# Preparing a recurrent segment inside the scan of the one before it, with both directions' outputs in one PSUM bank

## The chip, the cores and the metric

One core of one Trainium2 chip. The metric is device microseconds (us) of one execution; the time before is the median of 3 runs.

## The reference, cut to what matters

Two layers of a hybrid backbone, float32. Each layer: adaLN (`silu(c) @ w_ada`), one input projection `h @ w_in` for 256 context and 256 latent tokens, three head groups (retention, latent attention MLA, RWKV-7), and an output projection with LayerNorm. The change concerns RWKV-7, which runs in both directions:

```python
def step(state, inp):                      # per direction, head; state (v, k)
    r_t, w_t, k_t, v_t, a_t, b_t = inp     # a = -kk, b = kk * a_rate
    sa = einsum('dbhvk,dbhk->dbhv', state, a_t)
    state = state * w_t[..., None, :] + sa[..., :, None] * b_t[..., None, :] \
          + v_t[..., :, None] * k_t[..., None, :]
    return state, einsum('dbhvk,dbhk->dbhv', state, r_t)
```

The inputs need `tanh`/`exp` of two low-rank products (`w_lora`, `a_lora`), a unit key `kk / |kk|`, and cumulative products of the decay. The result is normalised per head.

## The kernel before, in words

TensorE (PE) runs in program order; the instructions of the other engines are put in order by a scheduler, which takes what is ready.

**Mainline.** All large projections (`pm`, L447; `acc`, L1311) and the 64 adaLN pieces (`adap`, L403, each with a load of 1 MB, tag `raw2`) form one list of pieces. A load brings `raw` (256 KB), ACT rounds it to `whi` (L225), POOL or DVE subtracts the rest `wlo` (L226), and PE multiplies three times. `ahead` runs ahead of PE in that list: `NRAW` = 10 pieces are loaded ahead (7 buffers), `NHI` = 4 of them split, and one adaLN piece more than the one in use (`raw2` has 2 buffers). The mainline is also PE's filler: `M(name)` adds the credit `FILL[layer][name]` (about us of PE time at the full clock) and issues mainline matmuls until it is used up. So filler moves matmuls from one place to another; their number stays.

**RWKV part.** For a layer, `rwkv_half` runs twice (4 of 8 heads each): unit keys (`sq`, `ss`, `nr`, with the reciprocal in L640), then two segments (context, latent), 8 segments in both layers. A segment has these steps:
1. Preparation, four units (direction d, head pair j): two matmuls `z`, four activations on ACT (`th`, `th`, `w`, `w`, L672 to L678), nine operations on DVE (two scans L681, `AR` L687 and L690 or L694, five that write `bf`, L698 to L705). Unit n+1 is emitted ahead of the gram of unit n, with filler `z0`, `gram`, `tp` between.
2. For each unit: `gram` matmuls (L711), mask to `G` on DVE (L714), `bs` on POOL (L718, one buffer), four transposes `bkT` (L723).
3. A block inverse on DVE: transposes to `Mt` (L747, copied by L148 on ACT), a chain of `stmp`/`S` pairs (L764, L767), transposes back, `TA` (L782), under filler `inv0` and `inv1`; then `pA`, `pB` on PE (L790).
4. The scan: 4 chunk steps, each a chain PE → ACT/DVE → PE: `xy` (L827, L846), copy `Y` (ACT, L148), `uz` (L852), copy `W`, `uz` (L861), new state `Zb` (DVE, L865 or L867), `xy` (L874); values of the next chunk (`uz` L816, `W` L820). `xy` and `uz` have a PSUM bank for each direction, which are all 4 banks of the pool `sm`.
5. Normalisation and output, deferred into the filler of the next segment (`norm`, `fin`).

Of the kernel before, what the change touches and what calls it, by code (L numbers as in the profile page):

```python
# [10 lines left out]
F32 = mybir.dt.float32  # L11
# [11 lines left out]
T = 512  # L23
# [114 lines left out]
def hybrid_kernel(ctx, tc, I, out, dbg=None, layers=L):  # L138
# [123 lines left out]
    def units():  # L262
        i = 0
        while True:
# [13 lines left out]
            ahead(i, loaded, False, NADA, lambda j: load(j, "raw2", NADA + 1))  # L278
# [341 lines left out]
    def rwkv_half(rp, l, hf, rF, kF, vF, twl, al, last):  # L620
        c0 = 2 * hf
        kkF = rp.tile([128, 2, T], F32, tag="kkF", name="kkF", bufs=1)
        w2t = rp.tile([128, 2, 256], F32, tag="w2t", name="w2t", bufs=1)
        for q, src in ((0, "rwkv_w2"), (1, "rwkv_a2")):
            nc.sync.dma_start(out=w2t[:, q, :],
                                in_=I[src][l].rearrange("d r c -> (d r) c")[:, 256 * hf:256 * hf + 256])

        M("begin")
        sq = []
        for j in range(2):  # L630
            sq.append(rp.tile([128, T], F32, tag="tb", name="sq", bufs=4))
# [12 lines left out]
        for d in range(2):
            for q in range(2):
                nc.gpsimd.memset(Zb[d][q], 0.0)
        Z = [None, None]
        for seg in range(2):
            need = not (last and seg == 0)
            NY = 128 if need else 64  # L650
            s0 = seg * NCTX
            AR, BK, G, pC = [], [], [], []
            Gt = rp.tile([128, 2, 4, 4, 128], F32, tag="G", name="G", bufs=1)
            for d in range(2):
                ar = rp.tile([128, 2, 4, 128], F32, tag="AR", name="AR", bufs=2)
                bk = rp.tile([128, 4, 2, 128], F32, tag="BK", name="BK", bufs=2)
                g = Gt[:, d]
                pc = rp.tile([128, 2, 4], F32, tag="pC", name="pC", bufs=2)
                AR.append(ar), BK.append(bk), G.append(g), pC.append(pc)
            def unit(d, j):  # L660
                ar, bk, g, pc = AR[d], BK[d], G[d], pC[d]
                mk = masks[:, d]
                fwd = (lambda ap: ap[:, ::-1]) if d else (lambda ap: ap)
                hp0 = 64 * d
                c = c0 + j
                cs = slice(j * 128, j * 128 + 128)
                sg = slice(s0, s0 + NCTX)
                z = pbank([128, 2, NCTX], "z")
                mm(z[:, 0], lhsT=w2t[hp0:hp0 + 64, 0, cs], rhs=twl[hp0:hp0 + 64, sg], start=True, stop=True)
                mm(z[:, 1], lhsT=w2t[hp0:hp0 + 64, 1, cs], rhs=al[hp0:hp0 + 64, sg], start=True, stop=True)  # L670
                th = rp.tile([128, 2, NCTX], F32, tag="tb", name="th", bufs=4)
                act(out=fwd(th[:, 0]), in_=z[:, 0], func=AF.Tanh, scale=0.5, bias=dpc(l, 14 + 4 * d + c))  # L672
                act(out=fwd(th[:, 1]), in_=z[:, 1], func=AF.Tanh, scale=0.5, bias=dpc(l, 22 + 4 * d + c))
                w = rp.tile([128, 2, 4, 65], F32, tag="w", name="w", bufs=2)
                nc.gpsimd.memset(w[:, :, :, 0], 0.0)
                thv = th[:, 0].rearrange("p (c t) -> p c t", t=64)
                act(out=w[:, 0, :, 1:65], in_=thv, func=AF.Exp, scale=-CDEC / 2, bias=val(0))
                act(out=w[:, 1, :, 1:65], in_=thv, func=AF.Exp, scale=CDEC / 2, bias=val(1))  # L678
                for q in range(2):
# [24 lines left out]
                TT(out=kx, in0=kx, in1=kn[:, ::-1, :] if d else kn, op=ALU.mult)
# [826 lines left out]
```

## Time and profile before

| | |
|---|---|
| Median of 3 runs (lowest, highest) | 2138.4 us (2136.77, 2141.34) |
| Profiled execution: time, span | 2137.61 us, 2135.8 us |
| PE, DVE, ACT, POOL busy | 92%, 60%, 38%, 29% |
| Mean granted TensorE clock | 0.949 of full speed |
| RWKV part of layer 0, layer 1 | 242 to 680 us, 1371 to 1810 us |

The profiled execution lies 0.8 us below the median; 1.8 us of it are outside the span. Busy shares are averages over stages with different limits.

### The profile page before, as it was taken

What the parts mean: (1) busy time and instruction counts of PE and PEld (TensorE: products, weight loads), DVE (VectorE), ACT (ScalarE), POOL (GpSimd) and SP (SyncE); (2) the same over time, 40 slices, a digit from 0 to 9 for tenths busy, and PEclk for the clock granted to TensorE, in tenths of its full rate; (3) what the DMA queues carried; (4) which work ended last, traced back from release to release, by engine and by line L of the source; (5) the groups of instructions that cost most, each with busy time, mean ns of one, the idle gap of its engine ahead of it and who ended that gap; (6) DMA issues with size and microseconds to landing.
All of it is one profiled execution on the core that took longest, in us unless ns stands there. A gap on an engine that the chain in (4) does not pass through costs nothing.

```text
span 2135.8 us, 35152 instructions
## 1 busy us (share of the span) xinstructions
PE 1959.7 (92%) x13046; PEld 1515.1 (71%) x13046; DVE 1273.4 (60%) x2985; ACT 813.1 (38%) x1559; POOL 611.3 (29%) x568
## 2 busy tenths in 40 slices
PE   6999999999989899999999979989798879899896
PEld 3567666676667577877877767766686668898775
DVE  2446876769493354446633374584749492466857
ACT  3223423343323344444322253423343234565442
POOL 0000433344243221112000055533444245513302
PEclk9999999999999999999999989978899889999998
DMA  9983442535243754536576533321322122743774
GB/s 338 352 272 98 143 141 71 163 114 173 75 148 106 256 160 124 158 104 231 183 249 230 179 104 108 99 55 31 87 75 80 39 75 74 206 111 111 237 242 157
DMA packets 255468, 318.42 MB, mean 149 GB/s; under 512 B 28288, under 2 KB 171968, under 8 KB 254400
## 3 DMA queue, kind: packets, MB, share of 16 engines
q1 hardware_dynamic: 255296, 316.16, 47.2%
q8 instruction: 103, 1.69, 0.3%
q14 instruction: 69, 0.57, 0.1%
HBM read 290.64 MB, written 25.46 MB: 148 GB/s over the span
## 4 chain that ended last, share of the span: by engine, by line
PE 46%; DVE 14%; ACT 2%; issue 1%; DMA 1%; POOL 0%; DVEq 0%; SPq 0%; ACTq 0%; POOLq 0%
PE pm L447 17%; PE acc L1311 11%; DVE stmp L764 2%; DVE S L767 2%; PE adap L403 1%; PE pj L344 1%; PE pj L343 1%; PE pj L342 1%; DVE H L583 1%; PE xy L827 1%; PE uz L852 1%; DVE G L772 1%; PE pmx L447 1%; PE gram L711 1%; PE pT L1123 1%
## 5 line engine op out<-in xcount | busy, mean ns | idle before, releaser
L447 PE MATMUL pm<-H,whi 128*128 128x512 f32 (+2 forms) x2880 | 853.6, 377 | 15.4 <-DVE stg L600 12.2
L226 POOL TENSOR_TENSOR wlo<-raw,whi 128x512 fp32r<-128x512 f32 x332 | 457.7, 1382 | 1078.1 <-ACT whi L225 992.0
L447 PEld LDWEIGHTS pm<-H,whi 128*128 128x128 f32 (+1 forms) x2880 | 520.7, 193 | 149.3 <-issue 43.3
L225 ACT ACTIVATE whi<-raw 128x512 fp32r<-128x512 f32 x556 | 348.9, 630 | 660.4 <-PE pm L447 316.7
L447 PE MATMUL pm<-H,wlo 128*128 128x512 f32 (+2 forms) x1440 | 541.3, 376 | 2.2 <-POOL wlo L226 2.2
L447 PEld LDWEIGHTS pm<-H,wlo 128*128 128x128 f32 (+1 forms) x1440 | 278.6, 193 | 57.6 <-issue 12.9
L226 DVE TENSOR_TENSOR wlo<-raw,whi 128x512 fp32r<-128x512 f32 x224 | 155.0, 695 | 201.5 <-ACT whi L225 162.5
L1311 PE MATMUL acc<-whi,Y 128*128 128x512 f32 x768 | 245.4, 399 | 5.0 <-DVE stg L600 4.6
L1311 PEld LDWEIGHTS acc<-whi,Y 128*128 128x128 f32 x768 | 143.3, 189 | 48.3 <-ACT whi L225 14.0
L1311 PE MATMUL acc<-wlo,Y 128*128 128x512 f32 x384 | 151.6, 395 | 0.0
L764 DVE TENSOR_TENSOR stmp<-S,Mt 128x60 f32<-128x60 f32 (+14 forms) x488 | 121.6, 289 | 6.5 <-ACT Mt L148 5.6
L767 DVE TENSOR_TENSOR S<-S,stmp 128x60 f32<-128x60 f32 (+14 forms) x488 | 108.0, 261 | 0.4
L447 PE MATMUL pmx<-H,whi 128*128 128x512 f32 (+1 forms) x256 | 87.1, 416 | 19.4 <-DVE H L583 13.0
L867 DVE TENSOR_TENSOR Zb<-Zc,uz 64x128 f32<-64x128 f32 x96 | 27.4, 286 | 126.1 <-PE uz L861 107.8
L1311 PEld LDWEIGHTS acc<-wlo,Y 128*128 128x128 f32 x384 | 72.5, 189 | 15.5 <-DVE wlo L226 0.4
L447 PEld LDWEIGHTS pmx<-H,whi 128*128 128x128 f32 x256 | 52.3, 215 | 37.5 <-DVE H L583 16.2
L148 ACT ACTIVATE Y<-xy 64x256 f32<-64x256 f32 x88 | 33.2, 377 | 118.5 <-PE xy L846 76.6
L403 PE MATMUL adap<-raw,scv 128*32 128x512 f32 x512 | 70.8, 626 | 0.0
L831 POOL TENSOR_TENSOR Zc<-Zb,pC 128x256 f32<-128x256 f32 x56 | 34.2, 615 | 118.0 <-DVE Zb L867 62.1
L711 PE MATMUL gram<-AR,bf 64*128 64x128 f32 (+1 forms) x512 | 42.9, 313 | 19.9 <-DVE bf L705 19.9
L711 PEld LDWEIGHTS gram<-AR,bf 64*128 64x128 f32 x512 | 36.8, 215 | 34.0 <-issue 21.3
L790 PE MATMUL pA<-TA,G 32*32 32x32 f32 x512 | 11.0, 237 | 54.0 <-DVE TA L782 54.0
(305 smaller groups left out, 2940.8 us busy)
## 6 DMA issues: line engine op xcount, KB each, us to landing
raw<-in_w_in SPq DMA_DIRECT2D x388, 256.0 KB, 2.8
raw<-in_w_ada SPq DMA_DIRECT2D x64, 1024.0 KB, 5.3
xraw<-in_w_ada SPq DMA_DIRECT2D x32, 1024.0 KB, 8.3
raw<-in_w_out SPq DMA_DIRECT2D x128, 256.0 KB, 4.0
raw<-in_mla_w_uq SPq DMA_DIRECT2D x48, 128.0 KB, 2.9
s_g<-stg SPq DMA_DIRECT2D x16, 256.0 KB, 3.1
gl<-s_g SPq DMA_DIRECT2D x16, 256.0 KB, 3.4
raw<-in_mla_w_ukv SPq DMA_DIRECT2D x32, 128.0 KB, 2.3
```

Of the source, the lines that this page charges most:

```text
L148: act(out=o, in_=i, func=AF.Copy)
L225: act(out=hi, in_=raw, func=AF.Copy)
L226: sub.tensor_tensor(out=lo, in0=raw, in1=hi.bitcast(F32), op=ALU.subtract)
L342: mm(ps, lhsT=ah, rhs=bh, start=first, stop=False)
L403: mm(st["ps"][32 * g:32 * g + 32, :], lhsT=sc(k + g), rhs=raw[:, g], start=(k == 0), stop=(k == KT - 4))
L447: mm(ps[p, i][:w], lhsT=x[:, o:o + w], rhs=H[y][:, a:], start=(k == k1 and n == 0), stop=(k == k2 - 1 and n == 2))
L711: mm(gps[p][:, i, :NY], lhsT=bf[hsl, i].rearrange("p a t -> p (a t)"), rhs=ar[hsl, j, i, :NY], start=True, stop=True)
L764: TT(out=tv, in0=S[:, r0:, s:s + 1].to_broadcast([128, n, b - a]), in1=Mt[s // 16][:, s % 16:s % 16 + 1, a:b].to_broadcast([128, n, b - a] ...
L767: TT(out=S[:, r0:, a:b], in0=S[:, r0:, a:b], in1=tv, op=ALU.add)
L831: nc.gpsimd.tensor_tensor(out=Zc[:, d], in0=Z[d], in1=pC[d][:, :, i:i + 1].to_broadcast([128, 2, 128]), op=ALU.mult)
L867: TT(out=Zn[hs(p), :, hs(p)], in0=Zc[hs(p), d, :, hs(p)], in1=zp[hs(p)], op=ALU.add)
L1311: mm(acc[cb, t], lhsT=Y[n][x][:, ts], rhs=y, start=(n == 0 and m == 0), stop=(n == KT - 1 and m == 2))
```

## The change

`rwkv` replaces both calls of `rwkv_half`. `prepare`, `grams`, `token_major`, `inverse_blocks`, `inverse_rest`, `scan`, `norm` and `finish` hold the code of the steps above. Only the first segment of a layer is prepared by itself. The four units of segment n+1 are emitted at hooks in the scan of segment n: within a half at A0, B0, B1, B2; between the halves at A1, B1, A2, B2, with the new half's `open_half` and `unit_keys` at S and A0. `norm` of a segment goes to A3 of the next scan. Hook A stands behind the copy `Y`, hook B behind `Zb` and `xy`.

To make a PSUM bank free for `z` and `ss` there, both directions' `xy` share one bank (`xyt`), and one copy of 64x512 (for two of 64x256) writes `Y` for both; so `uz` of either direction waits for both. `chain()` gives operations of the inverse and scan chains a higher priority in the scheduler. With `RP`, the second factor of `AR`, the last factor of `bf` and two operations of `norm` go from DVE to POOL. `bf` has 4 buffers of its own, `AR` and `pC` 4 (before 2), `Y` 2 (before 1); `NRAW` is 7 (4 buffers of `raw`), `raw2` has 1 buffer. The table `FILL` is new for the RWKV part.

```diff
 FILL = [
-    dict(zq=0.7, norm=2.34, end0=17.28, a0=3.38, a1=0.7, ada=2.41, begin=3.59, sq=2.6, nr=8.0, z0=3.35,
-         gram=1.84, tp=1.15, inv0=0.07, inv1=26.4, pA=1.2, pB=1.2, xy=0.39, u=0.44, zp=0.42, fin=15.02,
+    dict(zq=0.7, end0=17.28, a0=3.38, a1=0.7, ada=2.41, begin=3.59, sq=2.6, nr=8.0, z0=5.0,
+         gram=0.7, tp=0.4, inv0=0.07, inv1=29.0, pA=1.2, pB=1.2, xy=0.6, u=0.5, zp=0.5,
          kr=8.65, rss=3.69, rms=7.04, pj=1.74, rope=3.02, s0=5.05, s=0.47, av=1.41, s1=1.5, end=5.5, ret0=0.85,
          ret=2.09),
-    dict(zq=0.0, norm=11.89, end0=15.71, ada=6.79, begin=9.04, sq=1.32, nr=8.31, z0=4.0, gram=1.09, tp=0.1,
-         inv0=1.61, inv1=23.4, pA=1.2, pB=1.2, xy=0.68, u=0.39, zp=0.55, fin=4.57, kr=9.24, rss=1.71, rms=3.8,
+    dict(zq=0.2, end0=15.71, ada=6.79, begin=9.04, sq=1.32, nr=8.31, z0=5.0, gram=0.5, tp=0.3,
+         inv0=0.7, inv1=27.0, pA=1.2, pB=1.2, xy=0.68, u=0.45, zp=0.55, kr=9.24, rss=1.71, rms=3.8,
          pj=0.14, rope=2.75, s0=3.42, s=0.0, av=0.0, s1=0.49, end=0.82, ret0=0.45, ret=1.57),
 ]
-NRAW = 10
+NRAW = 7
+HPO = 300
+RP = True
 NHI = 4
...
-            ahead(i, loaded, False, NADA, lambda j: load(j, "raw2", NADA + 1))
+            ahead(i, loaded, False, NADA, lambda j: load(j, "raw2", 1))
...
+            STT(out=ar[:, j, :, 0:64], in0=Px, scalar=-1.0, in1=kkv, op0=ALU.mult, op1=ALU.mult)
+            PT = nc.gpsimd.tensor_tensor if RP else TT
+            if S.need:
+                if d == 0:
+                    PT(out=ar[:, j, :, 64:128], in0=Pi, in1=v4(rF[:, j, sg]), op=ALU.mult)
...
+            bf = S.bf[d, j] = rp.tile([128, 4, 2, 64], F32, tag="bf", name="bf", bufs=4)
...
+            PT(out=kx, in0=kx, in1=rn, op=ALU.mult)
...
+        def scan(S, hook):
+
+            rF, kF, vF = S.F
+            s0, need, AR, BK, pC = S.s0, S.need, S.AR, S.BK, S.pC
+            G = [S.G[:, d] for d in range(2)]
+            Y = S.Y = rp.tile([128, 4, 256], F32, tag="Y", name="Y", bufs=2)
             Yb = [rp.tile([128, 2, 256], F32, tag="tb", name="Yb", bufs=4) for n in range(2)] if need else None
             Zc = rp.tile([128, 2, 2, 128], F32, tag="bs", name="Zc", bufs=1)
-            hs = lambda h: slice(64 * h, 64 * h + 64)
-            xy = [pbank([128, 256], "xy") for d in range(2)]
+
+            xyt = pbank([128, 2, 256], "xy")
+            xy = [xyt[:, d] for d in range(2)]
...
+            hook("S")
...
-                    copy_a(Y[0:64, 2 * d + i % 2, :], xy[d][0:64])
+                                   start=False, stop=(d == 1 and j == 1 and r.start == 0))
+                with chain():
+                    copy_a(Y[0:64, i % 2::2, :], xyt[0:64])
+                hook(f"A{i}")
                 M("xy")
...
-                    copy_a(W[d][0:64], uz[d][0:64, 0:256])
+                    with chain():
+                        copy_a(W[d][0:64], uz[d][0:64, 0:256])
...
                 if i < 3:
+                    hook(f"B{i}")
                     M("zq")
...
+        def norm(S):
+            rF, kF, vF = S.F
+            Y, sg = S.Y, S.sg
+            yq = Y[64:128].rearrange("p c (h e) -> p (c h) e", e=64)
+            sm = rp.tile([128, 4, 16], F32, tag="gst", name="gst", bufs=1)
+            mean, var, rs = sm[64:128, 0], sm[64:128, 1], sm[64:128, 2]
+            PT = nc.gpsimd.tensor_tensor if RP else TT
+            nc.vector.tensor_reduce(out=mean, in_=yq, axis=AX.X, op=ALU.add)
+            TS(out=mean, in0=mean, scalar1=1.0 / 64, scalar2=None, op0=ALU.mult)
+            PT(out=yq, in0=yq, in1=mean.unsqueeze(2).to_broadcast([64, 16, 64]), op=ALU.subtract)
+            for n in range(0, 16, 8):
+                y2 = rp.tile([128, 8, 64], F32, tag="tb", name="y2", bufs=4)
+                act(out=y2[64:128], in_=yq[:, n:n + 8], func=AF.Square)
+                nc.vector.tensor_reduce(out=var[:, n:n + 8], in_=y2[64:128], axis=AX.X, op=ALU.add)
+            TS(out=var, in0=var, scalar1=1.0 / 64, scalar2=RW_EPS, op0=ALU.mult, op1=ALU.add)
...
+        M("begin")
+        open_half(0)
+        M("sq")
+        unit_keys(0)
+        M("nr")
+        S = Segment(0)
+        for d, j in ORDER:
+            prepare(S, d, j)
+            M("z0")
+        before, normed = None, None
+        for n in range(4):
...
+            copies = []
+            for d, j in ORDER:
+                bs = grams(S, d, j)
+                copies.append(lambda d=d, j=j, bs=bs: token_major(S, d, j, bs))
+                M("gram")
+                if len(copies) > 1:
+                    copies.pop(0)()
+                M("tp")
...
+            copies.pop()()
+            if normed:
+                finish(normed)
+                normed = None
+            M("inv1")
+            inverse_rest(S)
+            N, todo = Segment(n + 1) if n < 3 else None, {}
+            if N:
+                us = [lambda d=d, j=j: prepare(N, d, j) for d, j in ORDER]
+                if N.seg:
+                    todo = dict(zip(("A0", "B0", "B1", "B2"), us))
                 else:
-                    defer("norm", lambda norm=norm: defer("fin", norm(), "rw"), "rw")
+                    todo = dict(zip(("A1", "B1", "A2", "B2"), us))
+                    todo["S"] = lambda: open_half(N.hf)
+                    todo["A0"] = lambda: unit_keys(N.hf)
+            if before:
+                todo["A3"] = lambda: norm(before)
+            scan(S, lambda at: todo[at]() if at in todo else None)
+            normed, before = before, S if S.need else None
+            S = N
+        if normed:
+            finish(normed)
+        norm(before)
+        M("end0")
+        finish(before)
```

On PE, in the first scan of layer 0, the first chunk step was this (`pm` is filler):

```order
L827 MATMUL xy<-W,G 64x64 x16
L852 MATMUL uz<-Y,G 64x64 x8
L447 MATMUL pm<-H,whi 128x512 x2
L861 MATMUL uz<-W,BK 64x64 x8
L874 MATMUL xy<-W,G 64x64 x8
L447 MATMUL pm<-H,wlo 128x512
L447 MATMUL pm<-H,whi 128x512 x2
L447 MATMUL pm<-H,wlo 128x512
```

and is now:

```order
L842 MATMUL xy<-W,G 64x64 x16
L680 MATMUL z<-twl,w2t 128x256
L681 MATMUL z<-al,w2t 128x256
L449 MATMUL pm<-H,whi 128x512 x2
L449 MATMUL pm<-H,wlo 128x512
L871 MATMUL uz<-Y,G 64x64 x8
L449 MATMUL pm<-H,whi 128x512 x2
L881 MATMUL uz<-W,BK 64x64 x8
L895 MATMUL xy<-W,G 64x64 x8
L680 MATMUL z<-twl,w2t 128x256
L681 MATMUL z<-al,w2t 128x256
```

The matmuls `z` of two preparations of the next segment stand in one step, and the second `xy` is followed by `z` where it was followed by filler.

On DVE, in the same scan, between the copies `W` of the first chunks (`Zb` is the new state, for two directions):

```order
L820 COPY W<-uz 64x256 x2
L865 COPY Zb_1931<-uz 64x2x64 x2
L865 COPY Zb_1933<-uz 64x2x64 x2
L820 COPY W<-uz 64x256 x2
L867 TENSOR_TENSOR Zb_1932<-Zc,uz 64x2x64 x2
L867 TENSOR_TENSOR Zb_1934<-Zc,uz 64x2x64 x2
L820 COPY W<-uz 64x256 x2
```

and now:

```order
L709 SCALAR_TENSOR_TENSOR bf<-th,kkF 128x4x64
L714 TENSOR_SCALAR bf<-th,dpr_88 128x4x64
L692 SCALAR_TENSOR_TENSOR w<-w,cst 128x260 x2
L715 TENSOR_TENSOR bf<-bf,kF 128x4x64
L697 SCALAR_TENSOR_TENSOR AR<-w,kkF 128x4x64
L710 SCALAR_TENSOR_TENSOR bf<-bf,w 128x4x64
L886 COPY Zb_2145<-uz 64x2x64 x2
L886 COPY Zb_2147<-uz 64x2x64 x2
L835 COPY W<-uz 64x256
L709 SCALAR_TENSOR_TENSOR bf<-th,kkF 128x4x64
L714 TENSOR_SCALAR bf<-th,dpr_88 128x4x64
L835 COPY W<-uz 64x256
```

Operations of a preparation stand ahead of the state copies `Zb` and of each `W`.

On POOL, at the gram stage of layer 0's second segment, before (`gst` belongs to the norm of the segment before):

```order
L684 COPY pC<-w 128x4
L718 TENSOR_TENSOR bs<-bf,pC 128x512
L675 MEMSET w 128x8
L684 COPY pC<-w 128x4
L226 TENSOR_TENSOR wlo<-raw,whi 128x512
L675 MEMSET w 128x8
L718 TENSOR_TENSOR bs<-bf,pC 128x512
L226 TENSOR_TENSOR wlo<-raw,whi 128x512
L718 TENSOR_TENSOR bs<-bf,pC 128x512
L752 MEMSET S 128x512
```

and now:

```order
L695 COPY pC<-w 128x4
L705 TENSOR_TENSOR AR<-w,rF 128x4x64
L716 TENSOR_TENSOR bf<-bf,w 128x4x64
L686 MEMSET w 128x8
L734 TENSOR_TENSOR bs<-bf,pC 128x512
L228 TENSOR_TENSOR wlo<-raw,whi 128x512
L921 TENSOR_TENSOR Y<-Y,gst 64x1024
L734 TENSOR_TENSOR bs<-bf,pC 128x512 x2
L228 TENSOR_TENSOR wlo<-raw,whi 128x512
L734 TENSOR_TENSOR bs<-bf,pC 128x512
```

The `AR` and `bf` products and a 64x1024 operation of the norm stand in POOL's row, the latter between the first `bs` and the second.

## Rows read from the trace of the kernel before

**Rows 1.** The page, busy time, share and instructions of each engine.
```profile
PE 1959.7 (92%) x13046; PEld 1515.1 (71%) x13046; DVE 1273.4 (60%) x2985; ACT 813.1 (38%) x1559; POOL 611.3 (29%) x568
```

**Rows 2.** Waits of PE, RWKV part of layer 0 (242 to 680 us): total, times, longest.
```profile
PE pA L790 <- DVE TA L782: 16.3, 8, 4.1
PE gram L711 <- DVE bf L705: 6.6, 4, 2.3
```

**Rows 3.** Waits of PE, RWKV part of layer 1 (1371 to 1810 us).
```profile
PE pA L790 <- DVE TA L782: 37.7, 8, 11.3
PE gram L711 <- DVE bf L705: 13.2, 7, 2.9
PE pm L447 <- DVE stmp L764: 2.8, 1, 2.8
PE uz L816 <- DVE Zb L867: 2.6, 6, 0.6
```

**Rows 4.** Windows: us, busy of PE, PEld, DVE, ACT, POOL; clock; DMA share; GB/s.
```profile
242.00:680.00 438.00, 414.48 (x3623) 294.74 (x3622) 309.00 (x881) 157.69 (x326) 159.48 (x167) 0.95 0.40 124
1371.00:1810.00 439.00, 380.81 (x3269) 305.82 (x3269) 289.92 (x843) 158.58 (x322) 177.67 (x181) 0.89 0.23 64
425.00:450.00 25.00, 25.00 (x348) 19.32 (x345) 6.10 (x19) 10.05 (x24) 7.50 (x12) 1.00 0.20 64
```

**Rows 5.** Timeline of PE, layer 0: start us, us, line, operation, count, idle before.
```profile
267.73 1.16 PE L711 MATMUL gram<-AR,bf 64*128 64x128 f32 x16
...
288.97 1.07 PE L403 MATMUL adap<-raw,scv 128*32 128x512 f32 x8
...
295.63 1.06 PE L403 MATMUL adap<-raw,scv 128*32 128x512 f32 x8
...
299.49 0.61 PE L447 MATMUL pm<-H,whi 128*128 128x512 f32 x2
303.82 0.32 PE L790 MATMUL pA<-TA,G 32*32 32x32 f32 x4 [3.72 <-DVE TA L782]
...
306.00 1.05 PE L447 MATMUL pm<-H,whi 128*128 128x512 f32 x2
```

**Rows 6.** Timeline of PE, layer 1, one segment.
```profile
1497.61 1.16 PE L711 MATMUL gram<-AR,bf 64*128 64x128 f32 x16 [0.60 <-DVE bf L705]
...
1537.22 0.31 PE L790 MATMUL pA<-TA,G 32*32 32x32 f32 x4 [10.73 <-DVE TA L782]
```

**Rows 7.** Timeline of DVE, layer 0, first and last bf of a preparation, and a block-inverse pair.
```profile
246.33 0.42 DVE L698 SCALAR_TENSOR_TENSOR bf<-th,kkF 128x256 f32<-128x256 f32 x1 [0.92 <-ACT th L673]
...
249.51 0.42 DVE L705 TENSOR_TENSOR bf<-bf,w 128x256 f32<-128x256 f32 x1
...
281.36 1.45 DVE L764 TENSOR_TENSOR stmp<-S,Mt 128x66 f32<-128x66 f32 x2
282.73 0.35 DVE L767 TENSOR_TENSOR S<-S,stmp 128x66 f32<-128x66 f32 x2
```

**Rows 8.** Timeline of ACT, the four activations of one preparation, first and last.
```profile
344.92 0.47 ACT L672 ACTIVATE th<-z,dpr 128x256 f32<-128x256 f32 x1 [0.68 <-PE z L670]
...
346.05 0.51 ACT L678 ACTIVATE w<-th,cst 128x256 f32<-128x256 f32 x1
```

**Rows 9.** Lines of DVE, the reciprocals: count, busy, mean ns of one.
```profile
L640 DVE RECIPROCAL nr<-nr 128x512 f32<-128x512 f32 x8 | 26.8, 3347 | 0.1
```

**Rows 10.** Lines of POOL: count, busy us, mean ns, idle before and releasers.
```profile
L718 POOL TENSOR_TENSOR bs<-bf,pC 128x512 f32<-128x512 f32 x32 | 35.6, 1113 | 29.3 <-PE bkT L723 19.4 <-DVE bf L705 7.2 <-DVE G L714 1.8
L831 POOL TENSOR_TENSOR Zc<-Zb,pC 128x256 f32<-128x256 f32 x56 | 34.2, 615 | 118.0 <-DVE Zb L867 62.1 <-DVE G L772 35.5 <-DVE Zb L865 20.2
```

**Rows 11.** Timeline of SP, an adaLN load of layer 0.
```profile
290.10 0.37 SPq L268 DMA_DIRECT2D raw<-in_w_ada  x1
```

**Rows 12.** One source's view: the 27 adaLN loads in 242 to 680 us.
```profile
DMA to landing us min/median/max: 5.1/5.3/8.4
```

**Rows 13.** Timeline of POOL, layer 0, one subtraction of the weight split.
```profile
281.25 1.34 POOL L226 TENSOR_TENSOR wlo<-raw,whi 128x512 fp32r<-128x512 f32 x1 [2.93 <-ACT whi L225]
```

More of the change, by code (lines that the diff above doesn't have):

```diff
@@ new lines, in inverse_blocks @@
+                Mt[n] = m
+            W32 = rp.tile([128, 16, 32], F32, tag="bs", name="S", bufs=1)
+            nc.gpsimd.memset(W32, 0.0)
+            for q in range(2):
+                nc.gpsimd.memset(W32[64 * q:64 * q + 64].rearrange("p a b -> p (a b)")[:, q:512:34], 1.0)
+            with chain():
+                for s in range(31, 0, -1):
+                    r0 = s // 2
+                    n = 16 - r0
+                    tmp = rp.tile([128, 256], F32, tag="W", name="stmp", bufs=4)
+                    h = (s // 2 if s > 1 else 0) if CUT else 0
+                    parts = [(h, s), (0, h)] if h else [(0, s)]
+                    tvs = [tmp[:, n * a:n * b].rearrange("p (a b) -> p a b", b=b - a) for a, b in parts]
+                    for tv, (a, b) in zip(tvs, parts):
+                        TT(out=tv, in0=W32[:, r0:, s:s + 1].to_broadcast([128, n, b - a]),
+                           in1=Mt[s // 16][:, s % 16:s % 16 + 1, a:b].to_broadcast([128, n, b - a]), op=ALU.mult)
+                    for tv, (a, b) in zip(tvs, parts):
+                        TT(out=W32[:, r0:, a:b], in0=W32[:, r0:, a:b], in1=tv, op=ALU.add)
+                for b in range(2):
+                    bs = slice(32 * b, 32 * b + 32)
+                    for q in range(2):
+                        nc.vector.transpose(out=Gr[bs, :, bs].rearrange("p r t -> p t r")[:, q::2],
+                                            in_=W32[64 * q + 32 * b:64 * q + 32 * b + 32])
@@ L790, in quadrants @@
                         mm(ps[c // 2][qs[c], k], lhsT=lhs, rhs=rhs, start=True, stop=True)
-                for n in range(2):
-                    copy_a(target(n), ps[0][qs[n]])
-                    nc.vector.tensor_copy(out=target(2 + n), in_=ps[1][qs[2 + n]])
+                with chain():
+                    for n in range(2):
+                        copy_a(target(n), ps[0][qs[n]])
+                        nc.vector.tensor_copy(out=target(2 + n), in_=ps[1][qs[2 + n]])
                 M(name)
@@ L819, in values @@
                 W[d] = rp.tile([128, 256], F32, tag="W", name="W", bufs=4)
-                nc.vector.tensor_copy(out=W[d][64:128], in_=uz[d][64:128, 0:256])
+                with chain():
+                    nc.vector.tensor_copy(out=W[d][64:128], in_=uz[d][64:128, 0:256])
             halves = (slice(0, 64), slice(64, 128)) if need else (slice(0, 64),)
@@ L853, in rwkv_half @@
                            start=True, stop=True)
-                    copy_a(W[d][0:64], uz[d][0:64, 0:256])
+                    with chain():
+                        copy_a(W[d][0:64], uz[d][0:64, 0:256])
                 M("u")
-                if not (seg == 1 and i == 3):
+                if not (S.seg == 1 and i == 3):
                     for d in range(2):
@@ L874, in rwkv_half @@
                             mm(xy[d][64:128, hs(h)], lhsT=G[d][0:64, i, h, 64:128], rhs=W[d][0:64, hs(h)], start=False,
-                               stop=(h == 3))
+                               stop=(d == 1 and h == 3))
+                    for d in range(2):
                         c = 3 - i if d else i
@@ new lines, in finish @@
+        def finish(S):
+            vF, Y, sg, rkk, c0 = S.F[2], S.Y, S.sg, S.rkk, S.c0
+            yp = pbank([128, 2, 256], "yT")
+            for j in range(2):
+                for c in range(4):
+                    nc.tensor.transpose(yp[:, j, 64 * c:64 * c + 64], Y[64:128, c, 128 * j:128 * j + 128],
+                                        idn[64:128, 64:128])
+            bp = pbank([128, 2, NCTX], "bp")
+            for j in range(2):
+                mm(bp[:, j], lhsT=K("blk"), rhs=rkk[:, j], start=True, stop=True)
+            TT(out=rkk, in0=vF[:, :, sg], in1=bp, op=ALU.mult)
+            for j in range(2):
+                STT(out=rkk[:, j], in0=yp[:, j], scalar=dpc(l, 38 + c0 + j), in1=rkk[:, j], op0=ALU.mult,
+                    op1=ALU.add)
+            nc.sync.dma_start(out=scr["yw", l][c0:c0 + 2, :, sg].rearrange("k p t -> p k t"), in_=rkk)
@@ L1410, in layer @@
                 feats(l, fp, 1)
[L1411 to L1413 removed]
+            rwkv(rp, l, last)
             flush()
```

334 lines of the change are left out of this document (138 added, 196 removed).

## The prediction

> **What bounds the kernel now.** I read the page first: PE is busy 92% of the span, and no other engine comes near [rows 1]. So the kernel gains only where PE idles, runs at the lower clock, or does fewer matmuls, and the change leaves the number of matmuls as it is. Then the waits of PE in the two RWKV parts. In layer 0, PE waits 16.3 us at `pA` for `TA`, which ends the block inverse, and 6.6 us at `gram` for the last `bf` of a preparation [rows 2]. In layer 1 the same two places cost 37.7 and 13.2 us, and two small ones 2.8 and 2.6 us [rows 3]. The third view, the windows, gives the granted clock: 0.95 in the RWKV part of layer 0 and 0.89 in that of layer 1, but 1.00 inside a scan, where PE is busy for all of 25 us and DVE for only 6.1, ACT 10.1, POOL 7.5 [rows 4]. The timeline tells where the clock goes: ahead of a `pA` wait of 3.72 us a pair of `pm` matmuls took 0.61 us, behind it 1.05 us [rows 5]. The granted clock there is the lower of its two levels, 1.2 GHz in place of 2.4, after an idle stretch.
>
> So the RWKV part has three kinds of place: gram stages, where PE waits for a preparation; inverse stages, where filler runs out ahead of the DVE chain; and scans, where filler covers all.
>
> **The gram waits: gain 19.8.** With the preparation done in the scan before, the `gram` of 6 of 8 segments finds its inputs ready. The first segments of the layers get four fillers `z0` of 5.0, about 20 us, against four preparations of 249.51 + 0.42 - 246.33 = 3.6 us of DVE each [rows 7], 14.4 us. I take all 19.8 us (6.6 + 13.2). Bounds: 0, if the wait only moves to another operation of the stage, and 19.8.
>
> **The inverse waits: gain 21.** From the start of the last `gram` (267.73) to `pA` (303.82) lie 36.1 us in layer 0, 3.7 of it idle [rows 5]; in layer 1 1537.22 - 1497.61 = 39.6 us, 10.7 idle [rows 6]. The chain is on DVE and stays; the filler under it grows. Counting matmul columns at the full clock between the last `gram` and `pA` in the order of both kernels, it goes from 26.9 to 29.5 us in layer 0, from 24.3 to 27.5 in layer 1. Taken at face value over 4 segments each, that is 4 x 2.6 + 4 x 3.2 = 23.2 us. I take 21, since filler that is no longer slowed by the clock covers less. Bounds: 0 and 54 (16.3 + 37.7).
>
> **The two small waits: gain 5.4** (2.8 + 2.6), bounds 0 and 5.4: the first lies in a gram stage, the second becomes covered by the larger scan filler.
>
> **The clock: gain 18.** The RWKV windows lose 0.05 x 438 + 0.11 x 439 = 70 us of full clock [rows 4], which at half speed is 140 us of low clock. I estimate that 30 of these are idle (of 82 us idle in both windows). Of the other 110 us I take 60% for work whose time is set by columns, as the pair above is; the rest are small matmuls. Lost: 110 x 0.6 x 0.5 = 33 us. The waits at `gram` and `pA`, 73.8 us, shrink by 40.8, or 55%; 55% of 33 is 18. Bounds: 0, if any remaining wait lowers the clock as long, and 33.
>
> **The preparations in the scan: cost 17.** 24 preparations (6 segments x 4) move into scans. Their PE work is the same. Before, PE had filler beside them; now they sit between chain steps, on ACT (1.64 us from the first `th` to the end of the last `w` [rows 8]) and on DVE, whose rows are in order: in the order of after, `bf`, `w`, `AR` stand ahead of `Zb` and of each `W`. A chain operation behind them waits, and PE's next step waits for it. Three DVE operations of the chain meet a preparation in a step, and each waits for about half of one running operation (0.42 to 0.64 us [rows 7]), about 0.23: 0.7 us a preparation, 24 x 0.7 = 17. Lower bound 0: DVE is idle three quarters of a scan [rows 4] and filler may cover. Upper bound: all 3.6 us on the chain, 24 x 3.6 = 86. I am near the lower end, since three chunk steps lie in those 25 us, and a preparation of 3.6 us fits into a step of 8 us beside the 2 us that DVE has there.
>
> **The unit keys in the scan: cost 7.** In the second segment's scan of each layer stand two reciprocals of 3.35 us [rows 9], which can't be interrupted. I charge one a layer to the chain: 2 x 3.35 = 6.7. Bounds 0 and 13.4.
>
> **The gram stage on POOL: cost 9.** The fillers there go from 1.84 and 1.15 to 0.7 and 0.4 (layer 0). `bs` takes 1.11 us on POOL and has one buffer [rows 10]; so each `bkT` waits for its `bs`, and one `bs` for the transposes before. Where filler covered it, I charge one `bs` a segment: 8 x 1.1 = 8.9. In some segments the 64x1024 operation of the norm stands ahead of the second `bs` too. Bounds: 0 and 4 x 8 x 1.1 = 35.
>
> **Fewer load buffers: cost 7.** An adaLN load now goes out when the last piece has been read. In the trace one goes out at 290.10, right behind the piece that ended at 290.04 [rows 5, 11]; the next piece began at 295.63, so 5.5 us are there, and a load lands after 5.1 to 8.4 us, mostly 5.3 [rows 12]. In the order of after, 22 of the 64 pieces follow the one before within 5.55 us of matmul columns. I charge 0.3 us each, 6.6. Bounds 0 and 22 x 3 = 66. The raw loads keep 4 buffers, ahead of pieces of 256 KB that land in half of that; I price those at nothing, with PE's work on four split pieces as cover. A smaller prefetch also leaves less ahead of the first adaLN loads at the start; unpriced.
>
> **RP: nothing.** It takes 2 x 0.42 us off DVE and puts 2 x 0.62 us (by the nearest POOL operation of that size [rows 10]) on POOL, which is idle two thirds of the scan [rows 4]. Against it the trace shows a DVE pair of the block inverse at 281.36 that took 1.45 us, the next one 0.35, while POOL ran a subtraction from 281.25 to 282.59 [rows 7, 13]: 1.1 us lost to 1.34 us of POOL. At that ratio 48 operations of 0.62 us would cost DVE up to 24 us; the chain operations of the scan read PSUM and took 0.3 to 0.4 us each in the stretch that I read, beside POOL, so I price 0, with 24 as the bound. The Trainium skill, page "SBUF — State Buffer", section "SBUF: two separate sides", says that a GpSimd operation and a VectorE operation with two SBUF inputs lock a shared port pair, and that the loser waits for the whole instruction. The pair above agrees. By that rule, were all 48 blocked stretches on the chain, the sum below would be 2142 in place of 2113.
>
> **Shared PSUM bank: nothing beyond this.** `uz` of one direction waits for the `xy` of both, but one copy takes the place of two; filler `xy` is larger (0.39 to 0.6 in layer 0).
>
> **The filler that moved.** By the same count, 27 us of filler leave the RWKV parts for the MLA stages, at full clock: neither gain nor loss, since it is PE's work at either place.
>
> **The sum.** Gains 19.8 + 21 + 5.4 + 18 = 64.2; costs 17 + 6.7 + 8.9 + 6.6 = 39.2. Against the profiled time: 2137.6 - 25.0 = 2112.6; the median of the runs is 0.8 higher, so 2113 us.
>
> **Rivals.**
> - *The scans swallow it all (17%).* DVE is idle enough, loads land in time, `bs` is covered: costs near 0. Then 2137.6 - 64.2 = 2073, down to 2043 if three quarters of the `pA` waits and 30 us of clock come back too. For it: DVE 6.1 of 25 us busy in a scan [rows 4]. Against: in-order rows.
> - *The preparations lie on the scan chain (16%, slower).* In the scan, PE is busy 25 of 25 us only because filler just covers the chain; the place is the copy `W` and `Zb` behind a preparation on DVE. At 3.6 us each, 86 in place of 17, and the clock falls in the scans, so that its 18 is lost: 2112.6 + 69 + 18 = 2200; at 2.2 us, 2112.6 + 36 = 2149. With the clock's gain kept, it decides from (17 + 25) / 24 = 1.75 us a preparation.
> - *The single adaLN buffer (8%).* At 3 us for each of 22 pieces, 66 in place of 6.6: 2172. It decides from 31.6 / 22 = 1.4 us each. The median landing, 5.3 us, is just inside the gap [rows 12].
> - *No change that can be measured (7%).* Waits at `pA` and `gram` are replaced by as many in the scan; 2138. What a measurement of this kernel can tell from no change is about 0.2%, 4.3 us.
>
> **How the numbers follow.** The forecast, 2092 to 2133, has 52%. Faster by over 0.2%: the forecast and the first rival, 0.69; slower: the second and the third, 0.24; the same: the last, 0.07. The range for 8 in 10 takes the upper half of the first rival and the milder cases of the slower ones: 2062 to 2158.
>
> **What the profile of after would show.** Right: no wait of `gram` for `bf` outside the first segments; `pA` waits of about 33 us in all; a granted clock above 0.95 in layer 1's part; small new waits of `xy` and `uz` for `Y`, `W`, `Zb`. Wrong: waits at `uz` or `xy` of over 40 us, `adap` waiting for a DMA, or `bkT` waiting for `bs` by more than one `bs` a segment; in any of these the clock falls with them.

## The result and the profile after

The changed kernel takes 2164.3 us (median of 4 runs, 2157.3 to 2173.3): 1.012 of the time before, interval 1.0077 to 1.0162. It is slower; the forecast was 2113. The profiled execution took 2167.75 us. From its page, PE's share, and the clock in 40 slices (9 is 90% or more):

```profile
PE 1983.9 (92%) x13046; PEld 1530.3 (71%) x13046; DVE 1234.9 (57%) x2905; ACT 806.4 (37%) x1515; POOL 663.1 (31%) x636
...
PEclk9999999769999999999999989999969999999998
```

PE idles 181.8 us (2165.7 - 1983.9) against 176.1 before (2135.8 - 1959.7), so the waits only changed places; and it is busy 24 us longer with as many matmuls. The waits of PE over the whole span show what changed:

```profile
PE adap L405 <- DMA raw<-in_w_ada: 25.4, 8, 6.4
...
PE pA L798 <- DVE TA L790: 11.6, 4, 6.7
PE pm L449 <- ACT stg L592: 10.5, 1, 10.5
PE xy L842 <- DVE W L835: 9.4, 10, 3.1
PE bkT L741 <- POOL bs L734: 9.2, 11, 1.6
...
PE ss L649 <- ACT nr L651: 4.0, 2, 2.0
```

`pA` fell from 54 to 11.6 us and `gram` no longer waits for `bf` anywhere [rows 2, 3]. In their place stand the adaLN load, an eviction behind ACT, `xy` for `W`, and `bkT` for `bs`. The 24 us lie with the clock: a slice of 7 and one of 6 stand in the RWKV part of layer 0, one of 6 in that of layer 1. Windows from `pB` to the last `xy` of the first and second scan of layer 0, then of layer 1 (columns as in [rows 4]):

```profile
316.00:355.00 39.00, 38.28 (x494) 28.27 (x481) 22.14 (x54) 16.38 (x39) 17.68 (x25) 1.00 0.25 87
404.00:475.00 71.00, 60.91 (x482) 42.92 (x471) 32.71 (x59) 21.29 (x45) 24.99 (x33) 0.63 0.17 54
1477.00:1506.00 29.00, 28.67 (x295) 19.95 (x282) 19.92 (x47) 13.20 (x31) 13.50 (x20) 1.00 0.16 51
1565.00:1625.00 60.00, 54.84 (x496) 40.12 (x496) 30.23 (x57) 20.67 (x44) 17.86 (x28) 0.69 0.10 28
```

The first scans with preparations run as hoped, at the full clock. The second scans, which also hold the unit keys of the next half, take 71 and 60 us at 0.63 and 0.69. Before, these two took 34 and 33:

```profile
415.00:449.00 34.00, 34.00 (x486) 24.87 (x486) 7.44 (x22) 12.25 (x29) 8.77 (x13) 0.93 0.31 96
1541.00:1574.00 33.00, 33.00 (x504) 29.54 (x503) 7.43 (x22) 13.82 (x32) 12.50 (x16) 0.92 0.16 43
```

What stands in these two scans is told by DVE's timeline, first in layer 0, then in layer 1:

```profile
428.01 3.34 DVE L653 RECIPROCAL nr<-nr 128x512 f32<-128x512 f32 x1
431.38 0.77 DVE L835 COPY W<-uz 64x256 f32<-64x256 f32 x2
...
443.62 1.70 DVE L692 TENSOR_TENSOR_SCAN w<-w,cst 128x260 f32<-128x260 f32 x2
445.34 0.43 DVE L835 COPY W<-uz 64x256 f32<-64x256 f32 x1
...
1579.79 3.35 DVE L653 RECIPROCAL nr<-nr 128x512 f32<-128x512 f32 x1
1583.17 0.77 DVE L835 COPY W<-uz 64x256 f32<-64x256 f32 x2
```

The copies `W` at 431.38 and 1583.17 start when a reciprocal ends; the one at 445.34 starts when a preparation's two scans end. PE in the same two scans:

```profile
410.45 1.93 PE L405 MATMUL adap<-raw,scv 128*32 128x512 f32 x8 [4.05 <-DMA raw<-in_w_ada]
...
420.21 2.07 PE L649 MATMUL ss<-sq,cst 128*128 128x512 f32 x2 [2.02 <-ACT nr L651]
422.21 1.97 PE L871 MATMUL uz<-Y,G 64*64 64x64 f32 x16
...
436.04 1.14 PE L871 MATMUL uz<-Y,G 64*64 64x64 f32 x16
...
445.92 0.90 PE L842 MATMUL xy<-W,G 64*64 64x64 f32 x16 [3.00 <-DVE W L835]
...
1573.79 1.12 PE L649 MATMUL ss<-sq,cst 128*128 128x512 f32 x2 [2.02 <-ACT nr L651]
...
1583.75 1.97 PE L842 MATMUL xy<-W,G 64*64 64x64 f32 x32 [3.14 <-DVE W L835]
```

After the load's wait of 4 us and 2 us at the second `ss`, the 16 `uz` matmuls took 1.97 us; at 436.04, with the clock back, 1.14. The wait of 3 us at 445.92, behind the preparation on DVE, was followed by the low clock to the scan's end. In layer 1 no load is late. There the clock is still 1.00 behind the 2 us at `ss` (1575 to 1580 us); it falls with the 3.1 us behind the reciprocal, and stays low with PE busy throughout:

```profile
1585.00:1615.00 30.00, 30.00 (x204) 22.26 (x200) 12.53 (x31) 10.14 (x22) 9.11 (x17) 0.50 0.04 10
```

### The profile page after: what moved, and what is told of

It reads as the page before. It is cut to its first block, busy times and chain, and to the rows that moved or that the text cites. A ratio compares the mean times of both kernels' runs of the same rounds, so it can differ in the third digit from the quotient of the medians.

```text
span 2165.7 us, 34925 instructions
## 1 busy us (share of the span) xinstructions
PE 1983.9 (92%) x13046; PEld 1530.3 (71%) x13046; DVE 1234.9 (57%) x2905; ACT 806.4 (37%) x1515; POOL 663.1 (31%) x636
## 5 line engine op out<-in xcount | busy, mean ns | idle before, releaser
L449 PE MATMUL pm<-H,whi 128*128 128x512 f32 (+2 forms) x2880 | 858.4, 378 | 28.7 <-ACT stg L592 10.5
L228 POOL TENSOR_TENSOR wlo<-raw,whi 128x512 fp32r<-128x512 f32 x332 | 437.0, 1321 | 1064.3 <-ACT whi L227 972.3
L449 PEld LDWEIGHTS pm<-H,wlo 128*128 128x128 f32 (+1 forms) x1440 | 279.8, 194 | 61.1 <-issue 12.1
L771 DVE TENSOR_TENSOR stmp<-S,Mt 128x60 f32<-128x60 f32 (+14 forms) x488 | 117.1, 280 | 0.9 <-POOL S L760 0.7
L774 DVE TENSOR_TENSOR S<-S,stmp 128x60 f32<-128x60 f32 (+14 forms) x488 | 113.3, 272 | 0.4
L405 PE MATMUL adap<-raw,scv 128*32 128x512 f32 x512 | 72.8, 643 | 25.4 <-DMA raw<-in_w_ada 25.4
L150 ACT ACTIVATE Y<-xy 64x512 f32<-64x512 f32 (+1 forms) x56 | 28.0, 500 | 146.8 <-PE xy L863 90.8
L730 DVE TENSOR_TENSOR G<-gram,masks 128x512 f32<-128x512 f32 (+1 forms) x64 | 37.3, 620 | 37.1 <-PE gram L726 36.6
L842 PEld LDWEIGHTS xy<-W,G 64*64 64x64 f32 x896 | 37.4, 152 | 23.5 <-issue 15.6
L449 PE MATMUL pmx<-H,wlo 128*128 128x512 f32 (+1 forms) x128 | 51.6, 403 | 0.0
```

What stands on the lines that cost most here:

```text
L150: act(out=o, in_=i, func=AF.Copy)
L228: sub.tensor_tensor(out=lo, in0=raw, in1=hi.bitcast(F32), op=ALU.subtract)
L405: mm(st["ps"][32 * g:32 * g + 32, :], lhsT=sc(k + g), rhs=raw[:, g], start=(k == 0), stop=(k == KT - 4))
L449: mm(ps[p, i][:w], lhsT=x[:, o:o + w], rhs=H[y][:, a:], start=(k == k1 and n == 0), stop=(k == k2 - 1 and n == 2))
L730: TT(out=S.G[:, d, :, 2 * j + p, :NY], in0=gps[p][:, :, :NY], in1=mk[:, :NY].unsqueeze(1).to_broadcast([128, 4, NY]), op=ALU.mult)
L771: TT(out=tv, in0=W32[:, r0:, s:s + 1].to_broadcast([128, n, b - a]), in1=Mt[s // 16][:, s % 16:s % 16 + 1, a:b].to_broadcast([128, n, b - ...
```

## The experiments

All are timed against the kernel before on the same chip; the ratio has its 95% interval.

**e1: the load buffers alone, in the kernel before.**
```diff
-NRAW = 10
+NRAW = 7
-            ahead(i, loaded, False, NADA, lambda j: load(j, "raw2", NADA + 1))
+            ahead(i, loaded, False, NADA, lambda j: load(j, "raw2", 1))
```


> The kernel before with the load buffers of after alone (NRAW 7, one raw2). Theory 'loads': the single adaLN buffer is what turned the gain into a loss, through PE's waits for the load (25.4 us in the trace of after) and the clock behind them; then before becomes 25 to 50 us slower, 2165 to 2190 us, and PE waits at adap. Rival 'scan': the loss comes from the preparations between the chain steps, and the buffers cost no more than my 6.6 us: 2140 to 2147 us.


2157.3 us, ratio 1.0082 (1.0061 to 1.0103): between the two. The buffers cost some 18 us by themselves: 2.7 times my term, but less than the theory asked. Its waits:

```profile
PE adap L403 <- DMA raw<-in_w_ada: 8.8, 8, 4.9
...
PE pm L447 <- POOL wlo L226: 6.1, 5, 2.2
...
PE acc L1311 <- ACT whi L225: 3.0, 4, 1.5
```

Half of it stands at `adap`; splits that come later (`wlo` 6.1 for 2.2, `whi` 3.0 for 0.4) are another part, which I had priced at nothing.

**e2: after, with a quarter of each adaLN load.**
```diff
-                src = pieces[j][0]
+                src = pieces[j][0] if tag == "raw" else pieces[j][0][:, 0:1]
-                mm(..., rhs=raw[:, g], start=(k == 0), ...)
+                mm(..., rhs=raw[:, 0], start=(k == 0), ...)
```


> After, but of each of the 64 adaLN pieces only the first quarter is loaded (256 KB for 1 MB), and all its matmuls read that quarter: three quarters of these weights are left out, and the matmuls stay. Theory 'loads': the waits of adap (25.4 us) vanish and the clock comes back behind them: 2164 - 25 - 20, about 2120 us. Rival 'scan': only the 25 us of waits go, the clock in the scans stays low (about 0.6 in the second scan of layer 0): 2140 us or more.


2140.6 us, ratio 1.0003 (0.9983 to 1.0023): the loads are worth 24 us in after. But the second scans stayed at 0.69 and 0.69. In layer 0's the wait for the load is down to 1.4 us, and the clock is still 1.00 from 415 to 420 us; then PE waits 3.4 us at `xy` for the `W` behind the second reciprocal, and has 0.50 from 425 to 460. So a late load is not needed to lower the clock there.

**e3: after, preparations behind the scan.**
```diff
-                    todo = dict(zip(("A0", "B0", "B1", "B2"), us))   # and A1, B1, A2, B2
+            for u in us:         # behind scan(...), z0 = 3.5
+                u()
+                M("z0")
```


> After, with the four preparations of the next segment behind the scan in place of within it (filler z0 of 3.5 behind each); unit keys, shared bank, priorities, POOL operations and load buffers stay. Theory 'loads': placing them in the scan was worth the gram waits and their clock, so this is 10 to 30 us slower than after, 2175 to 2195. Rival 'scan': it takes the 9.4 us of xy waiting for W and the low clock out of the scans: 2130 to 2150.


2134.1 us, ratio 0.9988 (0.9965 to 1.0011): 30 us faster than after, as the rival said. "Loads" alone falls. The second scans, with the unit keys alone, take 43 us each at 0.88 and 0.82.

**e4: after, `sq` in the buffers of `bf`.**
```diff
-                sq = rp.tile([128, T], F32, tag="tb", name="sq", bufs=4)
+                sq = rp.tile([128, T], F32, tag="bf", name="sq", bufs=4)
```


> After, with the squares of the next half (sq) in the buffers of bf in place of tb. In the trace of after ACT waited 5.2 and 6.7 us at sq for the block inverse to free a tb buffer, and an eviction queued behind it held PE for 10.5 us (layer 1). If that block is a cost of its own, 8 to 18 us are won with the clock behind it: 2146 to 2156. If filler would only run out one step later, as the chain on DVE ends at the same time, nothing: 2164.


2159.5 us, ratio 1.0102 (1.008 to 1.0124), not to be told from after. The wait of 10.5 us for ACT is gone, and `pA` waits 22.8 us for 11.6: the blocked eviction lay in the time of the DVE chain.

**e5: e3 with two adaLN buffers** (`raw2` 2 buffers, `AR` 2).
```diff
-            ahead(i, loaded, False, NADA, lambda j: load(j, "raw2", 1))
+            ahead(i, loaded, False, NADA, lambda j: load(j, "raw2", NADA + 1))
```


> As e3 (preparations behind the scan), and the adaLN pieces have their two buffers back; AR needs only its 2 buffers there, which pays for it. If placement in the scan and the single buffer are two costs that add up, e3's 2134 falls by the 17.6 us that e1 showed for the buffers (less the part that NRAW 7 has in it): 2115 to 2122. If the two costs were one (the load waits only hurt where a scan is fragile), nothing: 2134.


2124.2 us, ratio 0.9938 (0.9915 to 0.996): 10 us; the costs add up in part.

**e6: after, hoisted within a half only.**
```diff
-                    todo = dict(zip(("A1", "B1", "A2", "B2"), us))
+            for u in us:         # these four behind the scan
+                u()
+                M(3.5)
```


> After, with the preparations within a half still in its first scan, but those of the second half's first segment (with filler of 3.5 each) behind the second scan. In the trace of after the low clock lies in the second scan of each layer (410 to 480 and 1580 to 1620 us), the one that also has the unit keys and three preparations in a row. If that scan alone is too full: as e3, 2130 to 2140. If any scan with preparations pays: half way, 2147 to 2152.


2130.7 us, ratio 0.9954 (0.9938 to 0.9969): the second scan alone carries the loss. With the keys still in it, it now took 52 us at 0.80 and 42 at 0.92. In layer 1 PE waits for the `W` behind the reciprocal as in after, 3.8 us for 3.1; but with no preparation behind it in the scan the clock is back some 5 us later, where after had 0.50 for 30 us and more:

```profile
1574.71 1.97 PE L842 MATMUL xy<-W,G 64*64 64x64 f32 x32 [3.84 <-DVE W L835]
...
1580.00:1599.00 19.00, 19.00 (x254) 15.04 (x254) 3.83 (x12) 6.24 (x15) 6.14 (x10) 0.99 0.10 29
```

So in layer 1 the keys start the low clock, and it lasts longer where preparations stand behind them. Why it does is not shown.

**e7 and e12: the kernel before with more filler under the inverse.**
```diff
-inv1=26.4   # layer 0; layer 1: inv1=23.4
+inv1=29.8   # layer 1: 31.0 in e7, 27.0 in e12
```


> The kernel before with more filler under the block inverse and nothing else: inv1 29.8 for 26.4 in layer 0, 31.0 for 23.4 in layer 1. My term for the pA waits says that filler there is worth its size and some clock: of 54 us at pA about 13 + 30 go, so 2139 - 43 - 10 of clock, about 2090 to 2100. Rival: more filler puts more subtractions of the weight split on POOL, which stretch the DVE chain (a pair 1.45 for 0.35 us), so half of it or less: 2115 to 2130.

> As e7, but inv1 27.0 in layer 1, as in after, in place of 31.0. e7 had 14.6, 11.4 and 9.9 us of new waits of pm for DVE and POOL in layer 1. If those came from the last 4 us of filler, this is faster than e7 (2117): 2105 to 2112; if the pA waits that come back cost as much: 2114 to 2122.


2117.2 us, 0.9895 (0.9879 to 0.9912), and 2117.3 us, 0.9909 (0.9881 to 0.9937). Filler under the inverse takes away `pA` waits, as my term has it, but for less than half the time that I expected of e7: of the 54 us at `pA`, 48 go in e7, and 22 us of time. In e7, `pm` waits 14.6 us once for an eviction on DVE and 11.4 for a split on POOL; with 4 us less filler (e12) those shrink and `pA` waits 21.8.

**e8: after, RP off.**
```diff
-RP = True
+RP = False
```


> After, with RP off: the second factor of AR, the last factor of bf and two operations of norm back on DVE. I priced the move at nothing: 2160 to 2168. If it is the moved operations that make the chain wait (bkT waited 9.2 us for bs on POOL, W for DVE), off is faster: 2145 to 2155. If DVE is what the scan lacks, off is slower: 2170 to 2185.


2165.5 us, ratio 1.0124 (1.0107 to 1.0142): nothing, as priced.

**e9: after, one preparation a step in the second scan.**
```diff
-                    todo = dict(zip(("A1", "B1", "A2", "B2"), us))
+                    todo = dict(zip(("B0", "B1", "B2", "A3"), us))   # norm behind A3
```


> After, with the four preparations of the second scan at B0, B1, B2 and A3 (one a chunk step) in place of A1, B1, A2, B2 (two a step). Unit keys stay in that scan. e6 showed that taking these four out is worth 33 us. If it is two in one step that makes W wait and drops the clock: 2135 to 2145. If preparations behind the unit keys cost the same wherever they stand: 2160 to 2168.


2142.7 us, ratio 1.0017 (1.0001 to 1.0032): crowding is part of it. The second scan of layer 1 runs at 1.00 again (42 us), that of layer 0 at 0.71.

**e10: after, unit keys of the second half ahead of the second segment's grams.**
```diff
+            if n == 1:
+                open_half(1)
+                M("sq")
+                unit_keys(1)
+                M("nr")
-                    todo["S"] = lambda: open_half(N.hf)
-                    todo["A0"] = lambda: unit_keys(N.hf)
```


> After, with the second half's unit keys (square, ss, reciprocal) ahead of the grams of the second segment, under fillers sq and nr, so that its scan holds preparations alone, at A1, B1, A2, B2 as before. If the 3.35 us reciprocals and the wait of ss (2.0 us) drop the clock and the preparations only keep it low: 2135 to 2145. If the preparations do it by themselves: 2158 to 2166.


2107.6 us, ratio 0.9861 (0.984 to 0.9882): the fastest kernel here, 57 us below after. The same four scans:

```profile
316.00:355.00 39.00, 38.13 (x487) 28.06 (x474) 22.91 (x53) 17.75 (x41) 17.17 (x25) 1.00 0.26 87
416.00:456.00 40.00, 37.56 (x501) 28.20 (x498) 24.52 (x52) 20.06 (x45) 19.86 (x30) 1.00 0.33 106
1443.00:1472.00 29.00, 28.66 (x309) 19.86 (x307) 19.41 (x46) 14.14 (x33) 13.52 (x20) 1.00 0.18 55
1542.00:1580.00 38.00, 37.11 (x494) 28.11 (x494) 21.31 (x50) 18.69 (x43) 16.21 (x27) 0.99 0.13 42
```

The second scans take 40 and 38 us for 71 and 60, which is 53 of the 57 us, with all four preparations still inside them. Two things move along with the keys: their fillers `sq` and `nr`, some 10 us a layer, and a load, for which PE waited 4 us at the start of layer 0's second scan in after and does not wait there now.

**e11: e6 with e4's buffers and adaLN loads in two tiles (three buffers, NRAW 5).**
```diff
-NRAW = 7
+NRAW = 5
+                    for q in (0, 2):
+                        t = wp.tile([128, 2, 512], F32, tag=tag, name=tag, bufs=bufs)
+                        dma(out=t, in_=src[:, q:q + 2])
```


> e6 (hoist within a half only) with the squares in the buffers of bf (e4) and the adaLN pieces loaded as two tiles of 512 KB with three buffers, NRAW 5. If the costs of e1, e4 and e6 add up: 2131 - 5 - 10 to 15, about 2113. If the smaller NRAW takes it back: 2125 to 2135.


2231.7 us, ratio 1.0444 (1.0419 to 1.047), a miss. `adap` hardly waits any more, but the splits come late everywhere:

```profile
PE pm L456 <- POOL wlo L228: 29.4, 23, 7.0
PE acc L1396 <- ACT whi L227: 23.2, 23, 2.3
PE pm L456 <- ACT whi L227: 22.8, 16, 7.2
```

**e13: after, without the two reciprocals of the second half.**
```diff
-                nc.vector.reciprocal(out=nr, in_=nr)
+                TS(out=nr, in0=nr, scalar1=0.0, scalar2=0.05, ...)   # second half
```


> After, but the two reciprocals of the second half's unit keys are left out (a short operation writes a constant in their place, so those keys are scaled by a constant). e10 showed that taking the unit keys out of the second scan is worth 57 us. If the 3.35 us reciprocals on DVE ahead of W are what does it: 2105 to 2125. If it is the wait of the second ss for its bank and the activations, which stay: 2150 to 2166.


2129.9 us, ratio 0.9953 (0.9933 to 0.9974): 34 us, between the two ranges. Second scans (in the profiled execution, which took 2143.6 us): 58 us at 0.79 and 40 at 1.00. In layer 0 the 0.50 stands from 410 to 430 us, behind a wait of 3.8 us for a load; from 435 us on the clock is 1.00.

**e14: after, the second `ss` and its key at B0.**
```diff
-                    todo["A0"] = lambda: unit_keys(N.hf)
+                    todo["A0"] = lambda: unit_keys(N.hf, (0,))
+                    todo["B0"] = lambda: unit_keys(N.hf, (1,))
```


> After, with the first ss and its key at A0 as now, the second at B0. No ss waits for the other's bank any more, and the reciprocals stand in different places of the scan, both still on DVE. If the 2.0 us wait of ss starts the low clock: 2105 to 2125. If the reciprocals do: 2145 to 2170.


2144.8 us, ratio 1.0019 (1.0006 to 1.0031): 20 us, less than the reciprocals. Second scans: 65 us at 0.79 and 41 at 1.00. So neither alone is the cause: in layer 1 changing either (or the crowding, e9) is enough, in layer 0 none is. There the late load has a part: at the start of that scan PE waits for it 4.1 us in e9, 3.8 in e13 and 5.3 in e14, each time with 0.50 behind it.

**e15: e3 with the keys out of the scan as in e10.** Its edit is e3's and e10's together.


> As e3 (preparations behind the scan with filler), and the second half's unit keys ahead of the second segment's grams as in e10, so that scans hold neither. If preparing within the scan is worth something by itself once the keys are out, this is slower than e10 (2108): 2118 to 2135. If filler behind the scan covers it as well: 2105 to 2115.


2145.3 us, ratio 1.0023 (1.0006 to 1.004): 38 us slower than e10, outside both ranges. With the keys out, preparing in the scan is better than preparing behind it under filler. A part shows after 1810 us: `rvT`, late in layer 1, waits 12.2 us for a load, as it does in e3, e5, e7 and e16 (11.4 to 11.8) and less in e12 (8.8), all of them with more filler in the RWKV parts than before; before and e10 have no such wait. That filler is missing at the end is argued from this, not shown. Why e15 is slower than e3 stays open.

**e16: e12 with more filler in the gram stage.**
```diff
-z0=3.35, gram=1.84   # layer 1: z0=4.0, gram=1.09
+z0=5.0, gram=2.5     # layer 1: z0=5.5, gram=2.6
```


> The kernel before with new numbers in its table alone: inv1 29.8 and 27.0 as in e12, and more filler in the gram stage (z0 5.0 and 5.5, gram 2.5 and 2.6) against the 17.4 us of gram waits left in e12. If filler buys what hoisting was to buy: 2117 - 17 + some, 2100 to 2108, as fast as e10. If the gram waits only move: 2114 to 2120.


2121.7 us, ratio 0.9905 (0.9885 to 0.9926): no more than e12. The `gram` waits for `bf` fell from 17.4 to 1.0 us, but `pT` waits 12.1 and `rvT` 11.7 us late in layer 1. That fits filler that is missing there, which is not shown.

**e17: e10 with adaLN loads in two tiles, two buffers.** e11's tiles, NRAW 7.


> e10 with each adaLN piece loaded as two tiles of 512 KB in two buffers (the same memory as one of 1 MB); NRAW stays 7. A half is free for the next load as soon as its matmuls are done. If e11's loss came from NRAW 5: 2100 to 2108, with less than e10's 14.5 us at adap. If the two tiles did it: 2150 or more.


2112.9 us, ratio 0.9859 (0.9801 to 0.9918): as e10. So the two tiles are harmless here, which leaves NRAW 5 (with 2 buffers of `raw` for 4) as the likely cause of e11's loss; it was not run by itself.

**e18: e10 without the chains' priority.**
```diff
-HPO = 300
+HPO = 0
```


> e10 with the scheduler's higher priority for the chain operations taken away (HPO 0). If the order that it gives on DVE and ACT is what lets preparations sit in a scan: 2120 to 2150. If the queues come out nearly alike: 2104 to 2112.


2109.4 us, ratio 0.9841 (0.9808 to 0.9875): with the keys out the priority changes nothing that can be measured.

## Why the prediction was wrong

- **The unit keys in the scan: this step failed.** I charged 7 us, at most 13.4, for reciprocals "which can't be interrupted", and nothing for a wait of the second `ss` or for what both do to the clock. Measured, with the preparations beside them: 57 us (e10, with the fillers and the load that move along); 34 of it go with the reciprocals alone (e13), 20 with the wait of `ss` and their distance alone (e14). The keys alone do not cost that much, and two terms that add up were the wrong form: the second scans took 34 and 33 us with neither (before), 40 and 38 with preparations (e10), 43 and 43 with keys (e3; 52 and 42 in e6, where a load is 4.7 us late in layer 0), and 71 and 60 with both. I had treated the clock as a gain of the stages before the scans, since a scan ran at 1.00, and not as something that the scan could lose. In the rival on the scan chain I let the clock fall, but at a price of 3.6 us for each of 24 preparations; it took only the two scans that hold the keys as well. That this rival's 2149 to 2200 holds the result is largely luck.
- **The preparations in the scan: 17 us forecast, hardly any where nothing else is added.** The first scans of the four halves took 39, 29, 39 and 31 us for 35, 28, 34 and 28 before, 13 us more for 16 preparations. But that is less than PE's own work on the matmuls `z` that came into them out of the gram stages, 4.5 us a scan and 18 in all; of `z` alone, in the first of these scans:

```profile
316.00:355.00 39.00, 4.51 (x16) 2.67 (x16) 0.00 (x0) 3.35 (x8) 0.00 (x0) 1.00 0.25 87
```

PE's waits in the four scans came to 2.2 us, against 4.8 before: the chain hardly waited for the preparations. Two to a step behind the keys they do cost: one to a step is worth 22 us (e9).
- **Fewer load buffers: 7 forecast, 18 (e1) to 24 (e2) measured.** The bounds (0 to 66) held it. The loads' waits came to 25.4 us at 8 pieces, not 0.3 each at 22, and the raw loads are not free (e1). `adap` waiting for a DMA was one of the prediction's own signs of being wrong.
- **The gram waits: right.** 19.8 forecast, and no wait for `bf` is left. The **`pA` waits** fell by 42, not 21, and e7 shows that 48 us of them are worth 22 of time, since PE then waits elsewhere. That 21 is near what they are worth in time is luck: twice the waits went, at half the price, and e7's 22 has the clock in it, which the forecast counted apart.
- **The gram stage on POOL: 9 forecast, 9.2 of waits measured** (`bkT` for `bs`); what they cost in time no run shows. **RP** at nothing was right (e8), and the scheduler's priority, which I had not priced, changes nothing either (e18). The shared bank alone was not tried.
- **The clock: 18 gained forecast.** The mean went from 0.949 to 0.942, with 0.93 for 0.95 in the RWKV part of layer 0 and 0.91 for 0.89 in that of layer 1. With the keys out (e10) the window 242 to 680 us has 1.00 and the other 0.93, so the term was there to be had.

An estimate of the whole from the terms: 2113, and 50 more for the keys, 11 to 17 more for the buffers and 17 less for the preparations, gives 2157 to 2163, against 2164 measured. It takes these as independent, which is not shown. A slip that changes nothing: by its own terms the lower end of the first rival is 2042, not 2043.

## What to carry to other kernels

Before work is put into a stage whose engine is full only because filler just covers a dependent chain, find the longest single operation that it brings to an in-order queue of that chain; here 3.35 us on DVE and a wait for one spare bank, beside preparations that were cheap by themselves, cost far more than either did alone. Price the stage at the lower clock too: here it lasted for 30 us and more. And count filler and buffers as a budget: what is spent in one stage (inverse filler, a load buffer) is missed in another.

## What the runs showed of the hardware

The clock did not come back soon in a scan: in after, five of the seven 10 us stretches from 410 to 480 us had 0.50 and the other two 0.81 and 0.87, with PE busy for 61 of 71 us of that scan; in layer 1 it had 0.50 from 1585 to 1615 us with PE busy for all 30. Elsewhere it came back sooner: in e6, behind a wait of 3.8 us in the same scan, by 1580 us, some 5 us later; before, behind the first `pA` wait, 0.50 stood from 304 to 314 us and 1.00 from 314 to 320. And four runs do not give a kernel's spread: before ranged over 4.6 us in the 4 runs beside after, and over 21 in the 7 beside e17.
